# Hybrid decoder layer on one core: weight-side sums of the seven-product pairs formed by accumulating GpSimd transfers on a second loaded copy, with the signs of one K block turned

## The chip, the cores and the metric

The kernel runs on one core of one Trainium2 chip. The metric is the device time of one execution in microseconds (us). Of the kernel before there are three runs: 1558.5, 1558.77 and 1559.57 us; the median is 1558.77 us.

## What is computed

One layer of a hybrid decoder on 256 tokens of width 4096, in float32. RMS-normed input goes through one wide projection (4096 x 12288, the columns of `IN_ORDER`), whose columns feed three mixers: causal pooling, stick-breaking attention with 16 heads, and a diagonal state-space branch with a small gated linear unit. The three branch outputs are normed, gated and concatenated to `y` (256 x 4096), and one output projection closes the layer:

```python
h = rmsnorm(x, ln_g)
proj = h @ w_in
...
y = jnp.concatenate([y_pool, y_attn, y_ssm], axis=-1)
h = x + y @ w_out
return rmsnorm(h, final_g)
```

The change lies in the product `y @ w_out` alone.

## The kernel before

All weights are streamed once. The stream is cut into 528 steps (`subs`); a step is a block of 256 K rows by 512 columns, loaded by one 512 KB transfer on the SP queue into a tile `w` (128 partitions x 2 x 512, four buffers, `load`, L135 to L138). Each float32 weight is split into a high and a low part so that TensorE's fast float32 mode keeps the accuracy: ScalarE writes `hi` (L94 or L228), VectorE writes `lo = w - hi` (L82). Products are then formed as three matmuls: high x high, high x low, low x high (`mm_tok`, L234 to L239, for 512 columns).

The stage at the end, the output projection, has eight units of 512 columns with 16 steps each; the 256 x 256 blocks of `y` are the stationary operands. An ordinary step takes 12 matmuls of 512 columns. Five steps of each unit, those in `SEVEN`, go another way: the two K tiles of 128 rows and the two halves of 256 columns are taken as a 2 x 2 block product and formed with seven products in place of eight (a Winograd form of Strassen's scheme). Such a step takes 21 matmuls of 256 columns (`mm_seven`, L169 to L185), and needs

- four sums of weight blocks, formed by VectorE in `sums_seven` (three operations on L82: one of 128 x 512 and two of 128 x 256 elements) from the loaded tile `w`, and split into high and low parts `sums7` (one ScalarE and one VectorE operation of 128 x 1024);
- three sums of blocks of `y`, formed once in `sums_of_rows` before the stage;
- a joining of four PSUM pieces at the end of each unit's last such step (`join_seven`, L187 to L195), which adds them into the residual tile `xr`.

The loop over steps is software-pipelined by emission order: in step i it emits the load of step i + 4 (`LOAD_AHEAD`), the split of step i + 2 (`SPLIT_AHEAD`), for a seven-product step its sums one step ahead of its split, and then the matmuls of step i. The `hi` and `lo` tiles have five buffers each, that is two and a half steps. A scheduler then sets the order on each compute engine from a timeline model; the SP queue keeps the order in which the program was written. GpSimd has no work but four small constants.

The tiles `t` (sums), `xr`, `e` (joining) and some others share one ring of six 4 KB-per-partition buffers (tag `k4`); `sums7` and others share a ring of three of 8 KB (`k8`). In the last unit, the last four steps (`HELD`) keep their split weights: the matmuls of the first token half run first, and those of the second half (`delayed`) run while the first half is being normed and stored.

Of the kernel before, what the change touches and what calls it, by code (L numbers as in the profile page):

```python
# [19 lines left out]
P = 128  # L20
L = 256
# [10 lines left out]
HELD = 4  # L32
SUMS_AHEAD = 1
SEVEN = (2, 5, 7, 9, 11)
SQUARE_AT = (0, 1, 3, 4, 6, 7, 9, 10)
# [20 lines left out]
def body(tc, a, out, ctx):  # L56
    nc = tc.nc
    V, S, T = nc.vector, nc.scalar, nc.tensor

# [60 lines left out]

# [1 line left out]
    wtiles, htiles = {}, {}  # L122
    held = []
# [34 lines left out]
    def split_seven(i):  # L158
        w = wtiles.pop(i)
        raw = []  # L160
        for kk in range(2):
            n = L if kk == 0 else NU
            hi = wp.tile([P, NU], F32R, tag="hi", bufs=5, name="hi")
            lo = wp.tile([P, NU], F32R, tag="lo", bufs=5, name="lo")
            hi_lo(hi[:, 0:n], lo[:, 0:n], w[:, kk, 0:n])
            raw.append((hi, lo))
        htiles[i] = (raw, htiles[i])

    def mm_seven(i, s, ps, pp):  # L169
# [5 lines left out]
        for o, stat, mov, begin, end in (  # L175
            (pp[0], xa[:, :, lo_half], [v[:, 0:L] for v in b11], first, last),
            (ps[:, 0, 0:L], xb[:, :, lo_half], [v[:, 0:L] for v in b2], False, False),
            (ps[:, 0, L:2 * L], y[:, 2], [v[:, L:2 * L] for v in b2], False, False),
            (pp[1], y[:, 0], [sums[:, h, 0] for h in range(2)], False, last),
            (pp[3], xa[:, :, hi_half], [sums[:, h, 1] for h in range(2)], first, last),  # L180
            (pp[2], y[:, 1], [sums[:, h, 2] for h in range(2)], False, last),
            (ps[:, 1, 0:L], xb[:, :, hi_half], [sums[:, h, 3] for h in range(2)], False, False),
        ):
            for k, (p, q) in enumerate(((0, 0), (0, 1), (1, 0))):
                T.matmul(o, stat[:, p, :], mov[q], start=begin and k == 0, stop=end and k == 2, skip_group_check=True)  # L185
# [10 lines left out]
    def sums_of_rows(qp, srcs):  # L196
        state["s7"] = {}
        for s in SEVEN:
# [49 lines left out]

# [1 line left out]
    state = {}  # L250
# [28 lines left out]

# [1 line left out]
    def log1pexp_parts(z, l):  # L281
# [47 lines left out]

# [1 line left out]
    pool_sums = cp.tile([P, 2, 2], F32, name="pool_sums")  # L331
# [43 lines left out]

# [1 line left out]
    uT = bp.tile([P, 8, L], F32, tag="k8", bufs=3, name="uT")  # L377
# [206 lines left out]

# [1 line left out]
    aout = {}  # L586
# [66 lines left out]

# [1 line left out]
    cur = {}  # L655
# [31 lines left out]

# [1 line left out]
    units = []  # L689
# [76 lines left out]
    def finish(kind, c, n, ps):  # L766
# [64 lines left out]
        elif kind == "ag":  # L831
            z = scaled(ps, "agz")
            if n == 2:
                drain(side_q)
                att_ctx.close()
                qp = ctx.enter_context(tc.tile_pool(name="rows", bufs=1, reuse_waits="tile"))
                side_q.append(sums_of_rows(qp, y_src))
            side_q.append(att_gate(lp, n, z))
            if n == 3:
                for i in range(28):  # L840
# [19 lines left out]
    for i, (ui, s) in enumerate(subs):  # L860
# [10 lines left out]
        while loaded < min(len(subs), i + 1 + LOAD_AHEAD):  # L871
            if loaded == 0:
                load_first()
            else:
                if loaded < KT // 2:
                    load_x(loaded)
                load(loaded)
            loaded += 1
        while split_to < min(len(subs), i + 1 + SPLIT_AHEAD):
            split(split_to)  # L880
            split_to += 1
            if seven(split_to + SUMS_AHEAD):
                sums_seven(split_to + SUMS_AHEAD)
        if s == 0:
# [156 lines left out]
```

## Time and profile before

| | us |
|---|---|
| median of three runs | 1558.77 |
| span of the profiled execution | 1556.4 |
| TensorE matmul busy | 1538.2 |
| VectorE busy | 1201.6 |
| ScalarE busy | 913.9 |
| GpSimd busy | 0.2 |
| data moved by DMA | 308.45 MB, 198 GB/s on average |

The span runs from the first to the last instruction of the profiled execution; the median of the runs is 2.4 us longer than this span. TensorE's busy time counts a matmul from its start to the modelled end of its pipeline, so 99% of the span says that matmuls follow one another without gaps, not that the array does peak work. Busy time of the other engines is true occupation. The output projection begins at about 1200 us of the span and TensorE's last matmul ends at about 1545 us; the rest is norm and stores.

### The profile page before, as it was taken

Reading aid. Unit: us, or ns where it says so; the run is one execution under the profiler, and the core shown is the slowest. Engines: PE = TensorE matmul, PEld = TensorE weight load, DVE = VectorE, ACT = ScalarE, POOL = GpSimd, SP = SyncE. Lnnn points to the kernel's source line nnn. Section 1 sums busy time; section 2 is a strip of 40 time slices with the busy share of each in tenths; the row PEclk is TensorE's granted clock in tenths of the full one; section 3 lists DMA queues with packets and bytes.
Section 4 is the critical chain, followed back from the end, with each engine's and each line's share of the span. In section 5 each row is a group of like instructions: output and inputs, shape, how many; then the busy total and the mean of one; then the engine's idle time right before and its main releaser. Section 6 shows DMA issues by size and latency. Waiting matters only on the chain.

```text
span 1556.4 us, 25428 instructions
## 1 busy us (share of the span) xinstructions
PE 1538.2 (99%) x9164; PEld 1360.9 (87%) x9164; DVE 1201.6 (77%) x2325; ACT 913.9 (59%) x1637; POOL 0.2 (0%) x4
## 2 busy tenths in 40 slices
PE   8999999999999999999999999999999999999996
PEld 8998788888799989998998889988888888888885
DVE  7579978999898879897556745455678888888886
ACT  7655556666565555565546754456667655555554
POOL 0000000000000000000000000000000000000000
PEclk9999999999999999999999999999999999999999
DMA  8866656566655546554555555545556666666665
GB/s 320 306 214 205 195 162 205 186 206 194 205 188 185 187 156 197 176 175 162 183 186 180 180 185 183 183 159 186 190 178 193 212 220 220 216 214 210 204 222 198
DMA packets 94079, 308.45 MB, mean 198 GB/s; under 512 B 11777, under 2 KB 17665, under 8 KB 93953
## 3 DMA queue, kind: packets, MB, share of 16 engines
q1 hardware_dynamic: 84096, 296.08, 58.2%
q10 hardware_dynamic: 9856, 10.76, 2.3%
q8 instruction: 71, 1.16, 0.3%
q14 instruction: 56, 0.45, 0.1%
HBM read 299.45 MB, written 4.19 MB: 195 GB/s over the span
## 4 chain that ended last, share of the span: by engine, by line
PE 96%; DVE 2%; DMA 1%; ACT 1%; issue 0%; SPq 0%; DVEq 0%; ACTq 0%
PE pm L238 18%; PE pm L237 18%; PE pm L239 18%; PE pm L245 10%; PE pm L247 10%; PE pm L246 10%; PE ps L185 3%; PE pm L185 3%; DVE lo L82 1%; PE ps_y L572 1%; DMA w<-in_ws 1%; PE ps_bu L545 0%; ACT hi L228 0%; PE ps_z L598 0%; PE ps_p L356 0%; PE ps_t L296 0%
## 5 line engine op out<-in xcount | busy, mean ns | idle before, releaser
L82 DVE TENSOR_TENSOR lo<-w,hi 128x512 fp32r<-128x512 f32 (+1 forms) x1048 | 696.9, 678 | 273.1 <-ACT hi L228 266.0
L228 ACT ACTIVATE hi<-w 128x512 fp32r<-128x512 f32 x968 | 604.6, 629 | 503.2 <-PE pm L239 204.4
L238 PE MATMUL pm<-lo,xhl 128*128 128x512 f32 x1232 | 482.4, 392 | 0.0
L239 PE MATMUL pm<-hi,xhl 128*128 128x512 f32 x1232 | 480.8, 390 | 0.0
L237 PE MATMUL pm<-hi,xhl 128*128 128x512 f32 x1232 | 480.6, 390 | 0.0
L245 PE MATMUL pm<-xhl,hi 128*128 128x256 f32 x1280 | 363.8, 284 | 5.3 <-ACT xhl L94 5.3
L246 PE MATMUL pm<-xhl,hi 128*128 128x256 f32 x1280 | 363.5, 284 | 0.0
L247 PE MATMUL pm<-xhl,lo 128*128 128x256 f32 x1280 | 363.4, 284 | 0.0
L238 PEld LDWEIGHTS pm<-lo,xhl 128*128 128x128 f32 x1232 | 231.5, 188 | 48.9 <-issue 2.1
L239 PEld LDWEIGHTS pm<-hi,xhl 128*128 128x128 f32 x1232 | 231.4, 188 | 47.3 <-issue 1.2
L237 PEld LDWEIGHTS pm<-hi,xhl 128*128 128x128 f32 x1232 | 231.5, 188 | 46.9 <-issue 0.4
L245 PEld LDWEIGHTS pm<-xhl,hi 128*128 128x128 f32 x1280 | 246.6, 193 | 7.1 <-ACT xhl L94 5.3
L247 PEld LDWEIGHTS pm<-xhl,lo 128*128 128x128 f32 x1280 | 246.6, 193 | 1.2 <-issue 0.8
L246 PEld LDWEIGHTS pm<-xhl,hi 128*128 128x128 f32 x1280 | 246.6, 193 | 0.8 <-issue 0.4
L91 DVE SCALAR_TENSOR_TENSOR et<-et,pw,tr 128x16 f32<-128x16 f32 (+3 forms) x256 | 55.6, 275 | 2.3 <-ACT tr L94 1.9
L94 ACT ACTIVATE sums<-t 128x1024 fp32r<-128x1024 f32 x40 | 42.3, 1058 | 23.8 <-DVE t L82 23.3
L82 DVE TENSOR_TENSOR sums<-t,sums 128x1024 fp32r<-128x1024 f32 x40 | 48.9, 1223 | 8.8 <-ACT sums L94 8.7
L94 ACT ACTIVATE hi<-w 128x256 fp32r<-128x256 f32 x80 | 40.0, 518 | 22.4 <-PE pm L239 18.9
L185 PE MATMUL ps<-sums,s 128*128 128x256 f32 x240 | 46.5, 283 | 1.1 <-DVE sums L82 1.1
L94 ACT ACTIVATE tr<-et,pw 128x32 f32<-128x32 f32 (+3 forms) x128 | 44.7, 384 | 4.7 <-DVE et L91 2.0
L82 DVE TENSOR_TENSOR t<-w 128x512 f32<-128x512 f32 x40 | 27.6, 690 | 24.3 <-DMA w<-in_ws 24.0
L560 DVE TENSOR_TENSOR_SCAN tb<-rho,ta 128x256 f32<-128x256 f32 x64 | 40.6, 676 | 0.1
(258 smaller groups left out, 1261.3 us busy)
## 6 DMA issues: line engine op xcount, KB each, us to landing
w<-in_ws SPq DMA_DIRECT2D x527, 512.0 KB, 3.5
xsq<-in_xr SPq DMA_DIRECT2D x8, 512.0 KB, 7.2
xr<-in_xr SPq DMA_DIRECT2D x8, 512.0 KB, 4.5
out<-o SPq DMA_DIRECT2D x8, 512.0 KB, 4.0
xt<-in_xT SPq DMA_DIRECT2D x15, 256.0 KB, 6.1
b<-in_bst ACTq DMA_DIRECT2D x16, 192.0 KB, 3.6
u<-uT ACTq DMA_DIRECT2D x96, 32.0 KB, 3.0
fg<-in_fg SPq DMA_DIRECT2D x8, 256.0 KB, 5.9
```

Source lines behind the costliest of these rows:

```text
L82: V.tensor_tensor(o, x, y, op)
L91: V.scalar_tensor_tensor(o, x, s, y, op0, op1)
L94: S.activation(o, x, f, **kw)
L185: T.matmul(o, stat[:, p, :], mov[q], start=begin and k == 0, stop=end and k == 2, skip_group_check=True)
L228: made = S.activation(hi, w[:, kk, :], AF.Copy)
L237: T.matmul(ps[t], stat[:, slot, 0, sl], hi, start=first, stop=False)
L238: T.matmul(ps[t], stat[:, slot, 0, sl], lo, start=False, stop=False)
L239: T.matmul(ps[t], stat[:, slot, 1, sl], hi, start=False, stop=last)
L245: T.matmul(o, hi[:, c], xhl[:, slot, 0, :], start=first and j % 2 == 0, stop=False, skip_group_check=True)
L246: T.matmul(o, hi[:, c], xhl[:, slot, 1, :], start=False, stop=False, skip_group_check=True)
L247: T.matmul(o, lo[:, c], xhl[:, slot, 0, :], start=False, stop=last, skip_group_check=True)
L560: V.tensor_tensor_scan(tb[:, c, :], rho[:, pr:pr + 1].broadcast_to([P, L]), ta[:, c, :], 0.0, ALU.mult, ALU.add)
```

## The change

The four weight sums are no longer formed by VectorE. Each seven-product step loads its 512 KB weight block a second time, on the SP queue, straight into the tile `t7`, eight steps ahead of its use (`SUMS_LOAD_AHEAD`). Three transfers issued by GpSimd then accumulate in place, each waiting for the one before: the right half of the weight block from memory onto the first two quarters of `t7` (256 KB), quarter 0 onto quarter 3 (128 KB), and quarter 3 onto quarter 2 (128 KB). An accumulating transfer can only add, so the differences of the old form are turned into sums by turning the sign of one K block: the sums over `y` rows and the joining take the signs, by scalar_tensor_tensor in place of tensor_tensor at two places each. The split into `sums7` stays and moves into `split_seven`, two steps ahead of use. Quarters 2 and 3 change places.

The seven-product steps are still five in each unit, at other places: (1, 4, 7, 10, 13) in place of (2, 5, 7, 9, 11). The row sums of step 13 need an output of attention that is ready later, so they are formed one block later. In the last unit step 13 is one of the last four; it runs for both token halves at once, so the `delayed` work is that of three steps in place of four.

```diff
-SUMS_AHEAD = 1
-SEVEN = (2, 5, 7, 9, 11)
+SUMS_LOAD_AHEAD = 8
+SEVEN = (1, 4, 7, 10, 13)
...
-    def sums_seven(i):
-        w = wtiles[i]
-        left, right = w[:, :, 0:L], w[:, :, L:2 * L]
+    def load_sums(i):
         t = bp.tile([P, 4, L], F32, tag="k4", bufs=6, name="t7")
-        tt(t[:, 0:2, :], right, w[:, 0, :].rearrange("p (c m) -> p c m", c=2), ALU.subtract)
-        tt(t[:, 2, :], right[:, 1, :], t[:, 0, :], ALU.subtract)
-        tt(t[:, 3, :], left[:, 1, :], t[:, 2, :], ALU.subtract)
+        nc.sync.dma_start(t.rearrange("p q m -> p (q m)").rearrange("p (k n) -> p k n", k=2), a["ws"][i])
+        G.dma_start(t[:, 0:2, :], a["ws"][i][:, :, L:2 * L], accum_op=ALU.add)
+        G.dma_start(t[:, 3, :], t[:, 0, :], accum_op=ALU.add)
+        G.dma_start(t[:, 2, :], t[:, 3, :], accum_op=ALU.add)
+        stiles[i] = t
+
+    def split_sums(i):
         sums = bp.tile([P, 2, 4, L], F32R, tag="k8", bufs=3, name="sums7")
-        hi_lo(sums[:, 0], sums[:, 1], t)
-        htiles[i] = sums
+        hi_lo(sums[:, 0], sums[:, 1], stiles.pop(i))
+        return sums
...
-        htiles[i] = (raw, htiles[i])
+        htiles[i] = (raw, split_sums(i))
...
-            (pp[2], y[:, 1], [sums[:, h, 2] for h in range(2)], False, last),
-            (ps[:, 1, 0:L], xb[:, :, hi_half], [sums[:, h, 3] for h in range(2)], False, False),
+            (pp[2], y[:, 1], [sums[:, h, 3] for h in range(2)], False, last),
+            (ps[:, 1, 0:L], xb[:, :, hi_half], [sums[:, h, 2] for h in range(2)], False, False),
...
-        tt(e[:, 1, :], e[:, 3, :], pp[1], ALU.add)
+        stt(e[:, 1, :], e[:, 3, :], -1.0, pp[1], ALU.mult, ALU.subtract)
         tt(e[:, 2, :], e[:, 3, :], pp[3], ALU.add)
-        tt(e[:, 3, :], e[:, 2, :], pp[1], ALU.add)
+        stt(e[:, 3, :], e[:, 2, :], -1.0, pp[1], ALU.mult, ALU.subtract)
...
-            tt(t[:, 0, :], xa[:, P:L], xb[:, P:L], ALU.add)
-            tt(t[:, 1, :], t[:, 0, :], xa[:, 0:P], ALU.subtract)
-            tt(t[:, 2, :], xb[:, 0:P], t[:, 1, :], ALU.subtract)
+            tt(t[:, 0, :], xb[:, P:L], xa[:, P:L], ALU.subtract)
+            stt(t[:, 1, :], t[:, 0, :], -1.0, xa[:, 0:P], ALU.mult, ALU.subtract)
+            tt(t[:, 2, :], xb[:, 0:P], t[:, 1, :], ALU.add)
...
+        if seven(i + SUMS_LOAD_AHEAD):
+            load_sums(i + SUMS_LOAD_AHEAD)
         while split_to < min(len(subs), i + 1 + SPLIT_AHEAD):
             split(split_to)
             split_to += 1
-            if seven(split_to + SUMS_AHEAD):
-                sums_seven(split_to + SUMS_AHEAD)
```

Two places of the built order show the moves. The first is the SP queue in the first units of the output projection. Before, it held weight loads with the residual and the final norm's gain once per unit (`w`, `xr`, `fg`):

```order
L137 DMA w_14570<-in_ws 128x1024
L761 DMA xr_14587<-in_xr 128x1024
L763 DMA fg_14589<-in_fg 128x512
L137 DMA w_14612<-in_ws 128x1024
L137 DMA w_14634<-in_ws 128x1024
```

Now a second copy stands between the weight loads, one after every three or four of them (`t7`):

```order
L149 DMA t7_13627<-in_ws 128x1024
L137 DMA w_13655<-in_ws 128x1024
L137 DMA w_13677<-in_ws 128x1024
L762 DMA xr_13687<-in_xr 128x1024
L764 DMA fg_13689<-in_fg 128x512
L137 DMA w_13712<-in_ws 128x1024
L137 DMA w_13737<-in_ws 128x1024
L149 DMA t7_13739<-in_ws 128x1024
L137 DMA w_13764<-in_ws 128x1024
```

Nothing else on SP moved: the loads of `w` keep their order.

The second is GpSimd's queue in the same stage, which was empty. L150 adds the right half of the weight block, L151 quarter 0 onto quarter 3, L152 quarter 3 onto quarter 2; the number names the tile:

```order
L150 DMA t7_13739<-in_ws 128x2x256
L152 DMA t7_13627<-t7_13627 128x256
L151 DMA t7_13739<-t7_13739 128x256
L150 DMA t7_13822<-in_ws 128x2x256
L152 DMA t7_13739<-t7_13739 128x256
L151 DMA t7_13822<-t7_13822 128x256
L150 DMA t7_13909<-in_ws 128x2x256
L152 DMA t7_13822<-t7_13822 128x256
L151 DMA t7_13909<-t7_13909 128x256
L152 DMA t7_13909<-t7_13909 128x256
```

The scheduler has put the first addition of the next tile between the second and the third of the present one; once in a unit the second and third of one tile stand together. Each L151 and L152 waits for the landing of its own tile's addition before it.

More of the change, by code (lines that the diff above doesn't have):

```diff
@@ L57, in body @@
     nc = tc.nc
-    V, S, T = nc.vector, nc.scalar, nc.tensor
+    V, S, T, G = nc.vector, nc.scalar, nc.tensor, nc.gpsimd
     ctx.enter_context(tc.manual_schedule(engines={mybir.EngineType.SP}))
@@ L119, in rsqrt_mean @@
         stt(dst, t, 1.5, dst, ALU.add, ALU.mult)
-    wtiles, htiles = {}, {}
+    wtiles, htiles, stiles = {}, {}, {}
     held = []
@@ L190, in join_seven, with sums_of_rows @@
         tt(e[:, 3, :], e[:, 0, :], pp[2], ALU.add)
-        tt(e[:, 1, :], e[:, 3, :], pp[1], ALU.add)
+        stt(e[:, 1, :], e[:, 3, :], -1.0, pp[1], ALU.mult, ALU.subtract)
         tt(e[:, 2, :], e[:, 3, :], pp[3], ALU.add)
-        tt(e[:, 3, :], e[:, 2, :], pp[1], ALU.add)
+        stt(e[:, 3, :], e[:, 2, :], -1.0, pp[1], ALU.mult, ALU.subtract)
         tt(xr, xr, e.rearrange("p (t c) m -> p t (c m)", t=2), ALU.add)
-    def sums_of_rows(qp, srcs):
-        state["s7"] = {}
-        for s in SEVEN:
+    def sums_of_rows(qp, srcs, which):
+        for s in which:
             xa, xb = srcs(2 * s), srcs(2 * s + 1)
             t = qp.tile([P, 3, P], F32, tag="t", bufs=1, name="ts")
-            tt(t[:, 0, :], xa[:, P:L], xb[:, P:L], ALU.add)
-            tt(t[:, 1, :], t[:, 0, :], xa[:, 0:P], ALU.subtract)
-            tt(t[:, 2, :], xb[:, 0:P], t[:, 1, :], ALU.subtract)
+            tt(t[:, 0, :], xb[:, P:L], xa[:, P:L], ALU.subtract)
+            stt(t[:, 1, :], t[:, 0, :], -1.0, xa[:, 0:P], ALU.mult, ALU.subtract)
+            tt(t[:, 2, :], xb[:, 0:P], t[:, 1, :], ALU.add)
             tt(xa[:, P:L], xa[:, 0:P], xa[:, P:L], ALU.subtract)
@@ L836, in finish @@
                 qp = ctx.enter_context(tc.tile_pool(name="rows", bufs=1, reuse_waits="tile"))
-                side_q.append(sums_of_rows(qp, y_src))
+                state["s7"] = {}
+                side_q.append(sums_of_rows(qp, y_src, [s for s in SEVEN if s < 12]))
             side_q.append(att_gate(lp, n, z))
+            if n == 2:
+                side_q.append(sums_of_rows(qp, y_src, [s for s in SEVEN if s >= 12]))
             if n == 3:
```

## The prediction

> **What bounds the kernel now.** I read the page first (busy shares, queues, the chain that ended last), then the waits of TensorE, then the stage of the change by windows.
>
> ```profile
> span 1556.4 us, 25428 instructions
> PE 1538.2 (99%) x9164; PEld 1360.9 (87%) x9164; DVE 1201.6 (77%) x2325; ACT 913.9 (59%) x1637; POOL 0.2 (0%) x4
> ...
> q1 hardware_dynamic: 84096, 296.08, 58.2%
> q10 hardware_dynamic: 9856, 10.76, 2.3%
> ...
> PE 96%; DVE 2%; DMA 1%; ACT 1%; issue 0%; SPq 0%; DVEq 0%; ACTq 0%
> ```
>
> TensorE makes 96% of the chain that ended last. The waits that end at its matmuls, over the whole span, are three:
>
> ```profile
> engine line waited for: us in total, times, longest us
> PE pm L245 <- ACT xhl L94: 5.3, 1, 5.3
> PE ps L185 <- DVE sums L82: 1.1, 1, 1.1
> PE pm L237 <- DVE o L82: 0.8, 1, 0.8
> ```
>
> The 5.3 us are the first load. Only 1.1 us, once in 40 seven-product steps, is a wait for weight sums: relieving VectorE can win little more than this. Now the stage, in stretches of about one unit each, and ahead of them a stretch near the start of the kernel (columns: PE, PEld, DVE, ACT, POOL busy, clock, share of the DMA engines, GB/s):
>
> ```profile
> core 0: us, PE busy (x) PEld busy (x) DVE busy (x) ACT busy (x) POOL busy (x), PEclk, DMA share, GB/s
> 8.00:24.00 16.00, 16.00 (x126) 16.00 (x125) 14.21 (x28) 13.47 (x28) 0.00 (x0) 1.00 1.03 401
> 24.00:50.00 26.00, 26.00 (x219) 26.00 (x219) 18.96 (x35) 17.99 (x35) 0.00 (x0) 1.00 0.86 286
> ...
> 1374.00:1417.00 43.00, 43.00 (x240) 37.66 (x239) 36.03 (x60) 24.79 (x42) 0.00 (x0) 1.00 0.65 214
> ```
>
> In the unit, TensorE is busy without a gap, VectorE for 36 of 43 us, and the DMA engines move 214 GB/s at a share of 0.65. Near the start the engines are full (1.03; packets overlap a little) and move 401 GB/s, and TensorE has no gap there either: heavy traffic by itself does not slow it. 401 GB/s is my capacity. The next 26 us, 286 GB/s at 0.86, would be 286 / 0.86 = 333 GB/s when full; this is the low end.
>
> The length of a unit comes from one instruction that stands once in each but the last (the final gain):
>
> ```profile
> L82 DVE TENSOR_TENSOR o<-o,fg x7: 1224/1225/1228, 1248.7 to 1505.1; 128x1024 f32<-128x1024 f32 x7
> ```
>
> Six intervals from 1248.7 to 1505.1 make 42.7 us a unit, 2.67 us a step.
>
> **The change, part by part.** *TensorE* keeps its work: five seven-product steps a unit before and now. Nothing is removed there.
>
> *VectorE* loses three operations a step (rows of the last 310 us, seven of the eight units):
>
> ```profile
> L82 DVE TENSOR_TENSOR t<-w,t 128x256 f32<-128x256 f32 x70 | 29.3, 419 | 0.2
> L82 DVE TENSOR_TENSOR t<-w 128x512 f32<-128x512 f32 x35 | 24.2, 690 | 20.5 <-DMA w<-in_ws 20.3
> ```
>
> 690 + 2 x 419 = 1528 ns, times 40 is 61 us of VectorE; off the path, so worth between 0 and the 1.1 us above. Four operations of the joining and of the row sums change their form from tensor_tensor to scalar_tensor_tensor: same sizes, a few tens of ns, hidden by VectorE's 7 idle us in a unit. ScalarE keeps its work.
>
> *DMA* is where the change costs. What a unit moves now: 16 loads of 512 KB, `xr` 512 KB, `fg` 256 KB:
>
> ```profile
> w<-in_ws SPq DMA_DIRECT2D x101, 512.0 KB, 3.9
> xr<-in_xr SPq DMA_DIRECT2D x6, 512.0 KB, 4.5
> fg<-in_fg SPq DMA_DIRECT2D x6, 256.0 KB, 5.9
> ```
>
> That is 9.18 MB, over 42.7 us 215 GB/s, as the window says. Added are five copies of 512 KB, 2.62 MB, and five times 256 + 128 + 128 KB accumulated, another 2.62 MB. The trace holds no accumulating transfer, so its price per byte is open. From below: like a copy. Then a unit has 14.42 MB, 338 GB/s over 42.7 us, 84% of 401: hidden, at no cost. From above: an accumulation reads the source, reads the old destination and writes, and each counts as a copy, so three times. Its pieces are of 1 KB; the queue with pieces of that order (q10, 1.1 KB a packet) moves 10.76 / 2.3 = 4.7 MB per percent of the engines against 5.1 on q1, so 9% more per byte. Three times: 9.18 + 2.62 + 3 x 2.62 x 1.09 = 20.4 MB, at 401 GB/s 50.8 us a unit, 8.1 over 42.7, times eight units 65 us. I take twice, the middle: the two reads pass one engine, the write goes out beside them. 9.18 + 2.62 + 5.71 = 17.5 MB, 43.7 us a unit: 1.0 us over TensorE's time, 8 us in the stage. That holds if the engines stay as full as in the 401 row; at half way to the low end, 367 GB/s, it is 47.7 us and +40 us in all. I take 1.6 us a unit, 13 us, nearer to the 401 row, because work then stands at the engines all the time, as there.
>
> The Trainium skill, "Collectives: The Full Stack", section "The bandwidth ceiling", gives a rule against this change: a reduce on a DMA engine has two source reads for each chunk on the same read ring, and its rate is half that of a copy (32.35 against 62.28 GB/s measured there). By the rule the price is twice a copy, which is the middle that I took; no transfer in this trace shows it.
>
> *The chain of transfers* behind each tile: second copy, then three accumulations, one after the other. Landing times nearest to them are 3.9 us (512 KB, above) and that of small copies within the on-chip memory:
>
> ```profile
> u<-uT ACTq DMA_DIRECT2D x96, 32.0 KB, 3.0
> ```
>
> Four landings are 12 to 16 us. The lead: the copy is issued eight steps ahead in a loop whose splits run as far ahead of TensorE at issue as at use, so 8 x 2.67 = 21.4 us. Hidden while landings stay under about 5 us. ScalarE's split of `t7` waits for the last landing; behind it in ScalarE's queue stand the `hi` parts of the next steps, for them VectorE's `lo` and TensorE.
>
> GpSimd's queue is in order. In the built order a tile's second and third addition have the first of the next tile between them, so a tile holds the queue for about two landings, 6 to 7.8 us, against 42.7 / 5 = 8.5 us of spacing. Hidden, with little to spare.
>
> *SP* gets 40 more issues at 0.33 us each (ns, window of one unit):
>
> ```profile
> L137 SPq DMA_DIRECT2D w<-in_ws x17: 327/328/328, 1373.9 to 1416.9; - x17
> ```
>
> They stand in a queue that mostly waits for a free `w` buffer; weight loads behind a second copy start that much later, hidden by their own lead of four steps, 10.7 us, against 3.9.
>
> *The tail.* In the last unit TensorE's end is followed by the norm; the joining now comes two steps later:
>
> ```profile
> 1535.77 0.19 PEld L238 LDWEIGHTS pm<-held,xhl 128*128 128x128 f32 x1 [0.26 <-DVE held L82]
> ...
> 1536.57 1.22 DVE L82 TENSOR_TENSOR xr<-xr,e 128x1024 f32<-128x1024 f32 x1
> 1536.71 0.19 PEld L238 LDWEIGHTS pm<-held,xhl 128*128 128x128 f32 x1 [0.41 <-DVE held L82]
> ...
> 1537.51 0.39 PE L238 MATMUL pm<-held,xhl 128*128 128x512 f32 x1
> ...
> 1537.74 0.40 PE L239 MATMUL pm<-held,xhl 128*128 128x512 f32 x1
> ...
> 1538.85 0.69 DVE L82 TENSOR_TENSOR o<-pm,xr 128x512 f32<-128x512 f32 x1 [1.06 <-PE pm L239]
> 1539.60 0.19 PEld L237 LDWEIGHTS pm<-held,xhl 128*128 128x128 f32 x1 [1.21 <-DVE o L82]
> ```
>
> ```profile
> L82 DVE TENSOR_TENSOR e<-e,ps 128x256 f32<-128x256 f32 x28 | 11.1, 417 | 2.3 <-PE ps L185 2.0
> ```
>
> Two waits for a late `lo` (0.26 and 0.41 us) go with VectorE's relief. After step 13, two steps of six matmuls remain before the first half is read, 12 x 0.23 = 2.8 us (the two starts above); the joining takes one copy, four operations of 0.42 us and the 1.22 us above, some 3.3 us, of which the copy runs under the last matmuls. I put the tail at zero, between -0.7 and +1.
>
> Sum against the profiled execution: 1556.4 + 13 + 0 = 1569.4 us; the runs lie 2.4 us above the span (1558.77 - 1556.4): 1571.8, say **1572 us**.
>
> **The rivals.** *Everything stays hidden (not slower).* One mechanism: an accumulation costs the engines less than 1.8 copies. It decides at the point where a unit's transfers fit in 42.7 us at 401 GB/s, 17.1 MB: (17.1 - 11.8) / (2.62 x 1.09) = 1.86; a little less with imperfect filling. For it: engines at 0.65 and a lead of 21 us; against it: 84% fill already at the lowest price. It gives 1558.3 us, with the tail and the 1.1 us wait between 1556.5 and 1560.
>
> *GpSimd's queue paces the stage.* Under load, or by generating descriptors in software, a landing takes 5 us: two per tile are 10 us against 8.5, 1.5 x 40 = 58 us, less the lead left over (21.4 - 15 = 6): +52, 1611 us. It decides from 8.5 / 2 = 4.3 us a landing. For it: `fg` lands in 5.9 us already; against it: the small copies' 3.0. The same time would come from an accumulation of three copies' price (+65).
>
> The Trainium skill, "DMA: Bandwidth & Descriptors", section "Anatomy of one DMA", fits a GpSimd transfer with 2.0 us + bytes / 436 GB/s; an estimate by it is 2.3 us for 128 KB, which would keep this rival away. No run here shows it, so it moves nothing in the numbers.
>
> *The change is a gain.* Only TensorE's 1.1 us and the tail's 0.7 are to be had: at most 1.8 us, 1557, which this measurement could not tell from no change (it tells about 0.2%, 3.1 us).
>
> **How the numbers follow.** Forecast, engines just over full: 0.43, own range 1563 (+4) to 1599 (+40). Far slower by GpSimd's queue or a triple price: 0.16. Hidden: 0.41, of which 0.05 for a gain over 0.2% by something in the stage that I don't see, 0.36 within. Slower by over 0.2%: 0.43 + 0.16 = 0.59. The range runs from the hidden case's low end, 1556, to 1612, which leaves out the gain (0.05) and the upper half of the far slower case (0.08 to 0.1).
>
> **What would show it.** Right: the DMA share in the stage at or above 0.95; TensorE with gaps in the units that end at weight loads or at `sums7`; units of about 44 us between two `o<-o,fg`. VectorE's busy time down by 61 us. Wrong towards hidden: units of 42.7 us, share below 0.9. Wrong towards far slower: units of 48 us and more, ScalarE waiting for `t7`, and landings of the L151 and L152 transfers over 4.3 us with the DMA share below 0.9 (queue) or at 1 (price).

## The result, and the profile after

| | before | after |
|---|---|---|
| median of four runs each, us | 1559.17 | 1680.55 (1679.41 to 1681.67) |
| ratio, 95% interval | | 1.078 (1.0764 to 1.0795) |
| span of the profiled execution, us | 1556.4 | 1679.0 |
| length of a unit in the last stage, us | 42.7 | 58.1 |

The change costs 121 us, nine times the forecast of 13. The page of the changed kernel: the span, the busy times, three DMA queues and the engines' shares of the chain that ended last.

```profile
span 1679.0 us, 25805 instructions
...
PE 1578.6 (94%) x9164; PEld 1382.8 (82%) x9164; DVE 1151.4 (69%) x2205; ACT 905.6 (54%) x1637; POOL 113.9 (7%) x124
...
q1 hardware_dynamic: 89856, 317.06, 55.5%
q0 software_dynamic: 22400, 20.98, 8.3%
...
PE 73%; DMA 15%; issue 5%; DVE 3%; ACT 2%; POOL 1%; SPq 0%; DVEq 0%; ACTq 0%; POOLq 0%
```

TensorE's part of the chain falls from 96% to 73%; DMA rises from 1% to 15%. The unit is read, as before, from the instruction that stands once in each unit but the last:

```profile
L82 DVE TENSOR_TENSOR o<-o,fg x7: 1216/1225/1226, 1268.8 to 1617.5; 128x1024 f32<-128x1024 f32 x7
```

(1617.5 - 1268.8) / 6 = 58.1 us. Eight units at 15.4 us more are 123 us: the whole loss lies in this stage. Two stretches of it by windows (PE, PEld, DVE, ACT, POOL busy, clock, DMA share, GB/s):

```profile
1350.00:1400.00 50.00, 39.57 (x195) 32.49 (x194) 25.61 (x38) 20.23 (x37) 13.06 (x14) 0.90 0.86 236
...
1450.00:1500.00 50.00, 38.06 (x184) 31.62 (x182) 20.06 (x31) 17.04 (x30) 12.15 (x13) 0.90 0.86 241
```

Every compute engine idles, the DMA engines are busy but not full (0.86 here, 0.84 to 0.94 in the eight stretches of 50 us from 1250 to 1650). Nothing is at its limit: that is the look of a stage held by latency. The waits of TensorE, of ScalarE (1200 to 1660 us), of GpSimd (1300 to 1500 us) and of SP (1240 to 1620 us) say where it is held:

```profile
PE ps L187 <- ACT sums L94: 51.6, 10, 7.6
PE pm L238 <- ACT hi L229: 10.2, 9, 2.1
PE ps L187 <- ACT hi L94: 7.9, 5, 4.8
PE ps L187 <- DVE sums L82: 4.5, 12, 0.5
```

```profile
ACT sums L94 <- DMA t<-t: 152.5, 27, 11.0
```

```profile
POOL t L151 <- DMA t<-in_ws: 75.0, 17, 8.4
POOL t L152 <- DMA t<-t: 37.8, 14, 7.0
POOL t L150 <- DVE lo L82: 23.8, 6, 7.5
POOL t L150 <- DMA t<-in_ws: 7.3, 4, 3.0
```

```profile
SPq L137 <- DVE lo L82: 304.7, 96, 13.3
```

TensorE waits for the split sums, and ScalarE for the landing that the sums are split from. GpSimd waits for its own landings (L151 and L152), but at L150 also for a second copy: these waits, those put down to `lo` too, end some 0.6 us after the copy's landing. In most of them the copy was already under way; in one GpSimd came free 0.7 us before SP issued it. SP stands at a weight load L137 that waits for `lo` to free a `w` buffer, 304.7 us of 380. That as such is nothing new; the kernel before, between 1240 and 1550 us:

```profile
SPq L137 <- DVE lo L82: 196.2, 85, 5.3
SPq L137 <- DVE t L82: 44.0, 21, 4.0
```

What is new is the longest such wait, 13.3 us in place of 5.3. One tile in the timeline ties the engines together:

```profile
1387.29 1.04 SPq L149 DMA_DIRECT2D t<-in_ws  x1
...
1392.93 1.08 POOL L150 DMA_DIRECT2D t<-in_ws  x1 [1.95 <-DMA t<-in_ws]
...
1398.21 0.89 POOL L151 DMA_DIRECT2D t<-t  x1 [4.19 <-DMA t<-in_ws]
...
1405.69 1.28 POOL L152 DMA_DIRECT2D t<-t  x1
...
1407.70 14.45 SPq L137 DMA_DIRECT2D w<-in_ws  x3
...
1417.07 1.06 ACT L94 ACTIVATE sums<-t 128x1024 fp32r<-128x1024 f32 x1 [10.12 <-DMA t<-t]
1418.04 2.17 ACT L229 ACTIVATE hi<-w 128x512 fp32r<-128x512 f32 x4
1418.18 0.58 PE L187 MATMUL ps<-sums,s 128*128 128x256 f32 x1 [6.75 <-ACT sums L94]
1419.30 2.83 DVE L82 TENSOR_TENSOR lo<-w,hi 128x512 fp32r<-128x512 f32 x5
1422.32 0.38 SPq L149 DMA_DIRECT2D t<-in_ws  x1
```

From the copy's issue at 1387.29 to the split at 1417.07 are 29.8 us; the forecast had 12 to 16 for four landings. While ScalarE stands at this split for 10.1 us, the `hi` of the next steps stands behind it; `lo` follows `hi`; the three weight loads that begin at 1407.70 are through only at 1422.15, when `lo` has freed their buffers; and the next second copy stands behind them and goes out at 1422.32. A late tile delays the next copies: the chain is a closed loop. The ring of `t7` buffers has no part in it: SP waited 0.4 us for one between 1240 and 1620 us. The landings themselves (medians of the whole program, issue to landing, in us):

```profile
w<-in_ws SPq DMA_DIRECT2D x527, 512.0 KB, 3.6
t<-in_ws SPq DMA_DIRECT2D x40, 512.0 KB, 6.5
t<-in_ws POOLq DMA_DIRECT2D x40, 256.0 KB, 6.3
t<-t POOLq DMA_DIRECT2D x80, 128.0 KB, 4.9
```

### The profile page after: what moved, and what is told of

Same layout as the page of the kernel before. It is cut to its first block, busy times and chain, and to the rows that moved or that the text cites. A ratio compares the mean times of both kernels' runs of the same rounds, so it can differ in the third digit from the quotient of the medians.

```text
span 1679.0 us, 25805 instructions
## 1 busy us (share of the span) xinstructions
PE 1578.6 (94%) x9164; PEld 1382.8 (82%) x9164; DVE 1151.4 (69%) x2205; ACT 905.6 (54%) x1637; POOL 113.9 (7%) x124
## 4 chain that ended last, share of the span: by engine, by line
PE 73%; DMA 15%; issue 5%; DVE 3%; ACT 2%; POOL 1%; SPq 0%; DVEq 0%; ACTq 0%; POOLq 0%
PE pm L239 13%; PE pm L240 13%; PE pm L238 13%; DMA t<-t 10%; PE pm L246 9%; PE pm L248 9%; PE pm L247 9%; DMA t<-in_ws 6%; DVE lo L82 2%; PE ps_y L573 1%; ACT sums L94 1%; ACT hi L229 1%; POOL t L150 1%; PE ps L187 1%; DVE sums L82 1%
## 5 line engine op out<-in xcount | busy, mean ns | idle before, releaser
L238 PE MATMUL pm<-hi,xhl 128*128 128x512 f32 x1236 | 487.5, 395 | 10.2 <-ACT hi L229 10.2
L239 PE MATMUL pm<-lo,xhl 128*128 128x512 f32 x1236 | 488.8, 395 | 3.7 <-DVE lo L82 3.3
L240 PE MATMUL pm<-hi,xhl 128*128 128x512 f32 x1236 | 485.4, 393 | 0.0
L238 PEld LDWEIGHTS pm<-hi,xhl 128*128 128x128 f32 x1236 | 235.2, 190 | 61.3 <-ACT hi L229 13.6
L239 PEld LDWEIGHTS pm<-lo,xhl 128*128 128x128 f32 x1236 | 234.9, 190 | 56.8 <-DVE lo L82 8.6
L240 PEld LDWEIGHTS pm<-hi,xhl 128*128 128x128 f32 x1236 | 234.2, 189 | 48.3 <-issue 1.2
L150 POOL DMA_DIRECT2D t<-in_ws x40 | 47.5, 1189 | 1273.2 <-DVE lo L82 1227.2
L187 PE MATMUL ps<-sums,s 128*128 128x256 f32 x240 | 57.5, 331 | 56.1 <-ACT sums L94 51.6
L187 PEld LDWEIGHTS ps<-sums,s 128*128 128x128 f32 x240 | 43.3, 224 | 61.4 <-ACT sums L94 53.7
L94 ACT ACTIVATE hi<-w 128x256 fp32r<-128x256 f32 x80 | 39.3, 514 | 40.3 <-PE pm L240 27.7
```

The source lines that it names most:

```text
L94: S.activation(o, x, f, **kw)
L150: G.dma_start(t[:, 0:2, :], a["ws"][i][:, :, L:2 * L], accum_op=ALU.add)
L238: T.matmul(ps[t], stat[:, slot, 0, sl], hi, start=first, stop=False)
L239: T.matmul(ps[t], stat[:, slot, 0, sl], lo, start=False, stop=False)
L240: T.matmul(ps[t], stat[:, slot, 1, sl], hi, start=False, stop=last)
```

## The experiments

Three theories stood against each other. A, **the loop of latency**: the copy's issue is tied to the splits, so a chain of some 28 us must pass within the steps that the lead spans, and sets the pace. B, **the engines' price**: the added bytes fill the DMA engines. C, **GpSimd's queue**: two landings a tile in one in-order queue set the pace. Thirteen kernels were run; the kernel before took 1558.0 to 1558.1 us beside them.

**The places alone.** The kernel before, with the five steps at the new places:

```diff
-SEVEN = (2, 5, 7, 9, 11)
+SEVEN = (1, 4, 7, 10, 13)
...
-                side_q.append(sums_of_rows(qp, y_src))
+                side_q.append(sums_of_rows(qp, y_src, [s for s in SEVEN if s < 12]))
...
+            if n == 2:
+                side_q.append(sums_of_rows(qp, y_src, [s for s in SEVEN if s >= 12]))
```

> The kernel before with the seven-product steps at the new places (1, 4, 7, 10, 13) and the row sums of step 13 one block later; the weight sums stay on VectorE. All theories: the places cost nothing, 1557 to 1562 us. Over 1570 us would say that a part of the loss is the places and the tail.

Measured: 1559.41 us, ratio 1.0011 (1.0001 to 1.002). The places, the tail with them, cost about 1 us.

**The traffic alone.** All added transfers run, but nobody waits for them: `sums7` is split from the plain weight block.

```diff
-        hi_lo(sums[:, 0], sums[:, 1], stiles.pop(i))
+        hi_lo(sums[:, 0], sums[:, 1], w.rearrange("p k n -> p (k n)").rearrange("p (q m) -> p q m", q=4))
```

> All transfers stay as in the changed kernel, but nobody waits for them: the operands called sums are the split of the plain weight block (the sums of weights are left out of what is computed; ScalarE, VectorE and TensorE do operations of the same number and size). Theory A: without the wait the loop is open; only the engines' traffic is left, 1562 to 1595 us. Theory B: the traffic itself costs it, 1660 to 1690 us. Theory C: as A, 1562 to 1595 us, since a late GpSimd queue only holds free tiles.

Measured: 1595.07 us, ratio 1.024 (1.0225 to 1.0256). The transfers as such are worth 37 us, and 85 us go when the wait for the sums goes. Its unit, a window, its queues q1 and q0 between 1200 and 1570 us, and a wait of SP:

```profile
L82 DVE TENSOR_TENSOR o<-o,fg x7: 1217/1225/1226, 1257.4 to 1540.3; 128x1024 f32<-128x1024 f32 x7
```

```profile
1350.00:1400.00 50.00, 45.75 (x249) 39.50 (x248) 31.80 (x47) 24.76 (x45) 16.43 (x18) 0.97 1.05 304
```

```profile
q1 hardware_dynamic: 25593, 91.11, 67.3%
q0 software_dynamic: 20601, 19.30, 33.3%
```

```profile
SPq L149 <- DMA t<-t: 81.6, 15, 8.3
```

The unit is 47.2 us and the DMA share 1.05, over 1300 to 1500 us 1.01: the engines are full. But SP also waits 82 us for tiles that the third accumulation has not left, so B and C are not told apart by this run alone.

**Plain transfers.** The same run with the three GpSimd transfers as copies:

```diff
-        G.dma_start(t[:, 0:2, :], a["ws"][i][:, :, L:2 * L], accum_op=ALU.add)
-        G.dma_start(t[:, 3, :], t[:, 0, :], accum_op=ALU.add)
-        G.dma_start(t[:, 2, :], t[:, 3, :], accum_op=ALU.add)
+        G.dma_start(t[:, 0:2, :], a["ws"][i][:, :, L:2 * L])
+        G.dma_start(t[:, 3, :], t[:, 0, :])
+        G.dma_start(t[:, 2, :], t[:, 3, :])
```

> As e3 (nobody waits for the second copies and the three transfers; the sums of weights are left out of what is computed), but the three transfers copy in place of accumulating: same bytes, same queue, same pieces. If an accumulation costs the engines about twice a copy, a unit's traffic falls from 47.1 us by half of the GpSimd queue's third of it, to about 39 us, and hides under TensorE's 42.7: 1557 to 1567 us. If bytes alone count: as e3, 1590 to 1600 us.

Measured: 1563.38 us, ratio 1.0033 (1.002 to 1.0047); the unit is back at 42.6 us. The same queue between 1200 and 1530 us:

```profile
q0 software_dynamic: 6631, 19.78, 16.9%
```

As many bytes take the engines half the time: 19.78 MB are 16.9% of 330 us, 55.8 us; accumulated, 19.30 MB were 33.3% of 370 us, 123.2 us. An accumulation costs (123.2 / 19.30) / (55.8 / 19.78) = 2.3 copies of the same blocks. The copies go in longer pieces (3.0 KB a packet against 0.9), and no run separates the two; the forecast's price of twice with pieces of 1 KB, 2.18, is close. Of the 37 us, 32 go with accumulating, the shorter pieces included, 4 with the bytes and 1 with the places.

**No chain between the accumulations.** The traffic alone, the second and third accumulation with sources that no transfer writes:

```diff
-        G.dma_start(t[:, 3, :], t[:, 0, :], accum_op=ALU.add)
-        G.dma_start(t[:, 2, :], t[:, 3, :], accum_op=ALU.add)
+        G.dma_start(t[:, 3, :], xhl[:, 0, 0, :].bitcast(F32), accum_op=ALU.add)
+        G.dma_start(t[:, 2, :], xhl[:, 1, 0, :].bitcast(F32), accum_op=ALU.add)
```

> The run of the traffic alone (nobody waits for the sums, which are left out), with the second and third accumulation made independent: they take 128 KB each from a resident tile of y parts (the same for all tiles) instead of the quarter that the accumulation before has just written. Bytes, pieces and issues are the same; of the waits in GpSimd's queue only that for the second copy is left. In the run of the traffic alone the queue waited 270 of 386 us for its own landings, SP 82 us for a tile that these had not yet left, and the DMA share stood at 1.0: queue or engines. Queue: without the waits the stage goes at TensorE's own pace, 42.7 us a unit, 1560 to 1572 us. Engines' price of accumulation: the same bytes, 46 to 48 us a unit, 1588 to 1600 us.

Measured: 1602.56 us, ratio 1.0285 (1.027 to 1.03). Its GpSimd waits between 1300 and 1500 us, its unit, a window, and a place ahead of the stage:

```profile
POOL t L150 <- DMA t<-in_ws: 110.5, 18, 13.6
POOL t L150 <- issue: 26.3, 3, 12.9
...
```

```profile
L82 DVE TENSOR_TENSOR o<-o,fg x7: 1225/1226/1226, 1266.0 to 1546.1; 128x1024 f32<-128x1024 f32 x7
```

```profile
1350.00:1400.00 50.00, 47.14 (x244) 38.23 (x243) 29.51 (x44) 23.53 (x44) 14.41 (x15) 1.00 1.04 302
```

```profile
1213.51 0.42 ACT L94 ACTIVATE xhl<-ypT 128x256 fp32r<-128x256 f32 x1 [6.56 <-DMA t<-xhl]
```

GpSimd no longer waits for any of its own landings, only for second copies, and the unit still takes 46.7 us at a share of 1.04. So the 37 us are the engines' price, not the queue. The median lies above the expected 1588 to 1600 because the run has a cost of its own: the writing of `xhl` waits once for transfers that read it, and TensorE waits 11.8 us for that.

**Lead of 12.** One number of the changed kernel:

```diff
-SUMS_LOAD_AHEAD = 8
+SUMS_LOAD_AHEAD = 12
```

> One number is changed: the second copy is issued 12 steps ahead of use in place of 8. In the changed kernel a tile needs 27 to 28 us from the issue of its second copy to ScalarE's split, and a unit takes 58.1 us, so that 8 of its 16 steps are 29 us. Theory A, a loop of latency: the issue of the second copy is tied to the progress of the splits, and a unit cannot be shorter than 16/8 of the chain. With 12 steps the chain allows 28 / 12 x 16 = 37 us a unit, under TensorE's 42.7; then the DMA engines bind at about 45 us a unit: 1575 to 1600 us. Theory B, the engines' price: the accumulations fill the DMA engines and no lead helps: 1665 to 1690 us. Theory C, GpSimd's in-order queue spends two or more landings per tile, about 11.6 us: no lead helps either, 1660 to 1690 us.

Measured: 1651.81 us, ratio 1.0605 (1.0587 to 1.0623): 29 us less, and outside the ranges of all three theories. It is far less than half as much lead again should bring: 28.4 us of chain in 12 steps would be hidden even at TensorE's pace (12 x 2.67 = 32 us).

**Two additions on VectorE.** The chain is cut to one accumulation:

```diff
-        G.dma_start(t[:, 3, :], t[:, 0, :], accum_op=ALU.add)
-        G.dma_start(t[:, 2, :], t[:, 3, :], accum_op=ALU.add)
...
+        tt(t[:, 3, :], t[:, 3, :], t[:, 0, :], ALU.add)
+        tt(t[:, 2, :], t[:, 2, :], t[:, 3, :], ALU.add)
```

> The second and third accumulation (128 KB each) are replaced by two VectorE additions of 128 x 256 just ahead of the split; the second copy and the first accumulation stay. Theory A: the chain is one copy and one accumulation, 6.6 + 1.1 + 6.5 = 14 us, under the lead of 21.4: 1558 to 1565 us. Theory B: half of the accumulated bytes go, the engines are at 86% of a unit at TensorE's pace: 1558 to 1575 us. Theory C: one transfer per tile on GpSimd: 1558 to 1565 us. All three expect a cure; a time over 1600 us would speak against all.

Measured: 1661.93 us, ratio 1.0666 (1.064 to 1.0691). The chain from copy to split fell from 28.3 to 15.4 us, yet only 19 us were won. All three theories had expected a cure: as they stood, all three failed here. Its timeline shows what waits for what:

```profile
1365.05 0.88 DVE L82 TENSOR_TENSOR t<-t 128x256 f32<-128x256 f32 x2 [8.96 <-DMA t<-in_ws]
1365.85 0.68 DVE L82 TENSOR_TENSOR lo<-w,hi 128x512 fp32r<-128x512 f32 x1
...
1366.59 0.79 PE L240 MATMUL pm<-lo,xhl 128*128 128x512 f32 x1 [5.20 <-DVE lo L82]
1367.18 0.63 PE L241 MATMUL pm<-hi,xhl 128*128 128x512 f32 x1
1367.61 0.63 PE L239 MATMUL pm<-hi,xhl 128*128 128x512 f32 x1
```

TensorE does not wait for the sums here but for a `lo` of an earlier step, which stands behind the addition on VectorE. In the built order of VectorE (the numbers name the tiles; `w_14023` is the block of the additions' own step):

```
L82 TENSOR_TENSOR lo_13944<-w_13881,hi_13943 128x512
L82 TENSOR_TENSOR t7_13905<-t7_13905 128x256
...
L82 TENSOR_TENSOR t7_13905<-t7_13905 128x256
L82 TENSOR_TENSOR lo_13965<-w_13903,hi_13964 128x512
...
L82 TENSOR_TENSOR lo_14082<-w_14023,hi_14081 128x256
```

The blocks 13903, 13937, 13962 and 13993 are split between the additions and their own step: the scheduler's model had the transfer land early and put the additions four steps ahead. A place ahead of its own step eats the lead, since an in-order engine makes earlier splits, and through SP the next copies, wait for it. So theory A, amended after this run, has to count the lead in the built order, not in the source. The same holds for the run before this one, where the sums stand 2.7 steps ahead on average.

**One transfer, additions behind their own split.** The run with two additions on VectorE, and one order constraint a tile: the first addition comes behind the split of its own step.

```diff
+            own = hi_lo(hi[:, 0:n], lo[:, 0:n], w[:, kk, 0:n])
...
+        behind(V.tensor_tensor(t[:, 3, :], t[:, 3, :], t[:, 0, :], ALU.add), own[1])
```

> As e2 (one accumulation, then two VectorE additions), but the additions are held behind the split of the tile's own step in VectorE's order; in e2's built order they stand 3.5 steps too early on average. Theory A, now with the lead counted in the built order: the loop runs from the split that frees a weight buffer, through the issue of the second copy behind that buffer's load, to the sums. In e2 it has about 4 to 4.5 steps for a chain of 15.4 us, which makes 56 us a unit, as measured (56.1). Behind its own step it has 8.5 steps: 31 us a unit, under TensorE's 42.7; the DMA engines are at about 39 of 42.7 us: 1558 to 1570 us. Theory B, price of the transfers alone: as e2, 1650 to 1670 us.

Measured: 1572.33 us, ratio 1.0089 (1.0074 to 1.0104): 90 us less by the order alone, with the same transfers and operations, and 2 us above the range of theory A. The waits of its TensorE in the stage, and ScalarE's wait at the sums for a landing (1200 to 1600 us):

```profile
PE ps L196 <- DVE sums L142: 7.1, 8, 0.9
...
PE ps L196 <- ACT sums L141: 3.3, 7, 0.5
```

```profile
ACT sums L141 <- DMA t<-in_ws: 0.8, 4, 0.2
```

ScalarE hardly waits for a landing any more. TensorE's 10.4 us, no longer than 0.9 each, and the 1 us of the places make most of the 14 that are left.

**Lead 12, and the sums' split behind its own step's.** The same constraint on the changed kernel, on ScalarE and VectorE, and the lead:

```diff
-SUMS_LOAD_AHEAD = 8
+SUMS_LOAD_AHEAD = 12
...
+        one, two = hi_lo(sums[:, 0], sums[:, 1], stiles.pop(i))
+        behind(one, own[0])
+        behind(two, own[1])
```

> As e1 (all three accumulations, second copy 12 steps ahead), but the split of the sums is held behind the split of its own step on ScalarE and VectorE; in e1's built order it stands 2.7 steps too early. Theory A: 12.5 steps for a chain of 29 to 31 us make 37 to 40 us a unit, so the loop no longer binds, and what is left is the engines' traffic as in e3 (47 us a unit): 1588 to 1610 us. Theory B: as e1, 1645 to 1660 us. Theory C (GpSimd's queue spends two landings a tile): as e1 too.

Measured: 1622.28 us, ratio 1.0406 (1.0362 to 1.045). Better than each alone, but 27 us over the traffic alone, and between the range of theory A and that of B and C. GpSimd's waits between 1300 and 1500 us:

```profile
POOL t L159 <- DMA t<-in_ws: 65.5, 20, 9.6
POOL t L160 <- DMA t<-t: 64.1, 17, 6.8
...
POOL t L158 <- DVE lo L82: 2.4, 2, 2.3
```

Now the queue hardly ever lacks a copy (L158 waits 2.4 us), and the chain has grown to 39.2 us, 17.3 of them from the copy's issue to the first accumulation's: theory C could be at work here. GpSimd works or waits for its own landings nearly all the time, as the engine that sets the pace would.

**GpSimd in program order.** The changed kernel, GpSimd's queue kept as written, three accumulations of a tile in a row:

```diff
-    ctx.enter_context(tc.manual_schedule(engines={mybir.EngineType.SP}))
+    ctx.enter_context(tc.manual_schedule(engines={mybir.EngineType.SP, mybir.EngineType.Pool}))
```

> The changed kernel with GpSimd's queue in the order of the program: the three transfers of a tile follow one another, with none of the next tile between them. Theory A: the chain of a tile loses the waits behind the next tile's first transfer, but a tile's first transfer then waits behind the third of the one before; the chain stays within 2 us of 28: 1660 to 1695 us. Theory C: the interleaving is the cause, under 1610 us; or, if three landings in a row bind the queue, 3 x 6 = 18 us a tile, 90 us a unit, over 1850 us.

Measured: 1724.96 us, ratio 1.107 (1.1039 to 1.11). Worse by 44 us, in none of the ranges: the first accumulation of a tile now waits behind two landings of the tile before (copy to first accumulation 15.7 us instead of 8.6), and the chain is 33.5 us. So the interleaving of two tiles, which looked like a danger, was a help; what the queue adds to the chain does count, more than A allowed for.

**Two additions on VectorE, with a lead of 12.** The run of that name, and:

```diff
-SUMS_LOAD_AHEAD = 8
+SUMS_LOAD_AHEAD = 12
```

> The run with two VectorE additions in place of the two accumulations inside the tile, and its lead raised from 8 to 12 steps. In the built order the additions then stand about 7.5 steps ahead of their own step's split (3.5 at a lead of 8), so that the loop still spans only about 4 steps. Loop of latency, counted in the built order: 16/4 x 15.5 us = 62 us a unit, no better than at a lead of 8: 1650 to 1720 us. Loop of latency with the lead counted as the source has it (12 steps for 15.5 us, far under the 32 us that 12 steps of TensorE take): 1560 to 1575 us. Engines' price alone (the transfers are those of the run at a lead of 8): as that run, 1655 to 1668 us.

Measured: 1663.85 us, ratio 1.0678 (1.0646 to 1.0709). Four steps more of lead bought nothing: the scheduler moved the additions four steps further ahead (7.5). The count by the source's lead is refuted; the count by the built order gave 62 us a unit and 55.4 were measured, so its size is rough where additions and split stand at different places on two engines.

**Lead 8, sums behind.** The constraint alone on the changed kernel, the lead as it was:

```diff
+        behind(one, own[0])
+        behind(two, own[1])
```

> The changed kernel with its lead of 8, and the split of the sums held in the built order behind its own step's split on ScalarE and on VectorE (mean place 1.3 instead of 0.55). Loop of latency: the loop spans 8.8 steps instead of 8.05; with the chain of 28.3 us unchanged that is 53 to 54 us a unit, 1630 to 1670 us. Engines' price, or the order without a part in it: 1675 to 1686 us.

Measured: 1666.63 us, ratio 1.0694 (1.0671 to 1.0716), 54.6 us a unit, just over the 53 to 54 that A had.

**Lead of 6.** One number of the changed kernel:

```diff
-SUMS_LOAD_AHEAD = 8
+SUMS_LOAD_AHEAD = 6
```

> The changed kernel with a lead of 6 steps instead of 8, nothing else (mean place of the sums 1.45). Loop of latency: the loop spans about 7 steps; 16/7 x 29.3 us = 67 to 68 us a unit, 9 to 10 us more in each of eight units: 1740 to 1790 us. Engines' price: the same transfers, 1675 to 1690 us.

Measured: 1723.1 us, ratio 1.1085 (1.1045 to 1.1124), 64.2 us a unit. Slower as A had it, and by 17 us less than its low end: the transfers of a slower stage land sooner, and the chain was 25.1 us instead of 28.3.

**GpSimd's queue in rounds.** Lead 12 and the sums behind, GpSimd in program order, written so that no accumulation waits for one issued just before it:

```diff
...
         G.dma_start(t[:, 0:2, :], a["ws"][i][:, :, L:2 * L], accum_op=ALU.add)
-        G.dma_start(t[:, 3, :], t[:, 0, :], accum_op=ALU.add)
-        G.dma_start(t[:, 2, :], t[:, 3, :], accum_op=ALU.add)
+        if chain:
+            second(chain[-1])
+        if len(chain) > 1:
+            third(chain.pop(0))
+        chain.append(t)
...
```

> The run with a lead of 12 and the sums' split behind their own step's, with GpSimd's queue written in rounds: first accumulation of a tile, second of the tile before, third of the one before that, so that each waits for a landing that began a whole round earlier. Same transfers, same sums. In the run without rounds the queue never lacked work and gave 10.2 us a tile (51.2 us a unit). Queue paces that run: a round costs one landing, 8.5 us, instead of 10.2; 43 to 47 us a unit, 1565 to 1600 us. Engines' price: not under the run of the traffic alone, 1592 to 1625 us. Loop of latency alone: the chain grows by the rounds to some 40 us over a loop of 12.8 steps, 50 us a unit: 1615 to 1640 us, no gain.

Measured: 1632.39 us, ratio 1.0488 (1.0467 to 1.0508). GpSimd between 1300 and 1500 us:

```profile
POOL t L167 <- DMA t<-in_ws: 67.6, 9, 11.0
...
POOL t L158 <- DMA t<-in_ws: 0.7, 1, 0.7
```

At L167, the first accumulation, it waits for second copies (144 us of the 200 with the rows left out here), and no longer for its own landings (0.7 us), and nothing is won: a landing was traded for a wait in the round, and the chain is 39.3 us as before; the unit is 52.3 us against 51.2. So theory C does not set the pace of this run, nor that of the changed kernel: its queue was left without a copy at times, and with a lead of 6 the stage was slower though the queue had the same work. For the run with a lead of 12 and the sums behind it is not excluded: there the queue hardly lacked work, and this run, which frees the queue, adds a wait of its own to the chain.

**Seven runs in one reckoning.** In a closed loop, the chain passes once in as many steps as lie between the split that lets a copy go and the split that uses it. Those are the lead, plus the place of the sums' split in the built order (1 right behind its own step's split, negative ahead of it), less half a step; the half is set so that the changed kernel comes out. The chain is the mean over tiles 4 to 37 from the copy's issue on SP to the split on ScalarE, as in the timeline above (29.8 us for that tile), plus 1 us for the split. A unit is 16 steps.

| run | lead | place | steps | chain, us | 16 / steps x (chain + 1) | unit measured |
|---|---|---|---|---|---|---|
| after | 8 | 0.55 | 8.05 | 28.3 | 58.2 | 58.1 |
| lead 12 | 12 | -2.7 | 8.8 | 28.4 | 53.5 | 53.9 |
| lead 8, behind | 8 | 1.3 | 8.8 | 28.9 | 54.4 | 54.6 |
| lead 6 | 6 | 1.2 | 6.7 | 25.1 | 62.3 | 64.2 |
| GpSimd in turn | 8 | 1.05 | 8.55 | 33.5 | 64.6 | 64.5 |
| lead 12, behind | 12 | 1.0 | 12.5 | 39.2 | 51.5 | 51.2 |
| in rounds | 12 | 1.2 | 12.7 | 39.3 | 50.8 | 52.3 |

The place of the run with a lead of 6 is counted in the order of ScalarE's instructions in its trace (the expectation had 1.45). By the same count the runs with two additions on VectorE have places of -2.7 and, with a lead of 12, -6.0, and chains of 15.4 and 16.5 us: 54.7 and 50.9 us a unit, where 56.1 and 55.4 were measured. So for these two the reckoning is rougher.

The table can't show by itself that the chain sets the pace. The time from a copy's issue to its use is the number of steps between them times the length of a step, in every loop whose copies go out with the steps. The run with the additions behind their own split shows it: place 1.6, 9.1 steps, 23.2 us from copy to split, 42.5 us by the table's formula and 44.6 measured, though ScalarE did not wait there and the accumulation had landed 7.9 us before the split. That the chain binds is shown by ScalarE's waits for the landing (152.5 us against 0.8) and by the runs that changed the order or the lead alone. Why a chain is as long as it is, is left open: a chain grew where the lead grew (39 us at 12 steps), and no run separates, in it, the fuller engines from tiles that queue behind each other.

## Why the prediction was wrong, step by step

*TensorE bound, VectorE's relief worth nothing:* right. The three operations are gone, VectorE's busy total fell by 50.2 us (1201.6 to 1151.4; the sum of the removed durations was 61, and busy time counts instructions that overlap once), and nothing came of it. The four operations that changed form cost nothing: `e<-e,ps` takes 419 ns in the new form and 414 in the old.

*DMA, an accumulation at twice a copy:* the price was nearly right (2.3 measured against copies in longer pieces, 2.18 forecast with the pieces), the sum too small. The forecast was 13 us, from a unit of 44.3 us. The traffic alone gave 37 and 47.2 (with the run without a chain: 46.7). The term that was mis-sized is what full engines move: they were about as full as in the 401 row (shares of 1.01 and 1.04 over 1300 to 1500 us against 1.03), but 17.5 MB by the forecast's own count in 46.7 to 47.2 us are 371 to 375 GB/s, not 401. Both parts of the sum took more: an accumulated MB 6.4 us of the engines (123.2 / 19.30) where the forecast had 2.18 x 1.03 / 401 GB/s = 5.6, and a loaded MB 2.7 us (67.3% of 370 us for 91.11 MB) where it had 2.57. In a unit that is 2 us each, at 2.62 and 11.8 MB. The forecast's "half way to the low end, 367 GB/s, it is 47.7 us and +40 us" was the better value. The Trainium skill, "Collectives: The Full Stack", section "The bandwidth ceiling", has a reduce at half the rate of a copy because both its sources are read; the runs with and without accumulation come near it, at 2.3 against its 1.9 (62.28 / 32.35), the shorter pieces included.

*The chain of transfers:* the step that failed. "Four landings are 12 to 16 us. The lead ... 21.4 us. Hidden while landings stay under about 5 us." Three things were wrong in it. The landings were taken from rows of the kernel before (3.0 and 3.9 us), whose stage had a DMA share of 0.65, though the step before it had just filled the engines: by the medians the four took 6.5 + 6.3 + 4.9 + 4.9 = 22.6 us, over the lead already (in the mean of 28.3 us, 24.9 are landings). The waits between them on GpSimd and ScalarE, 3.4 us in that mean, were left out. And the lead was taken as a fixed time, out of which only the excess would be paid; but the copy is issued behind weight loads that wait for `lo`, and `lo` stands behind the late sums. In such a loop nothing is given back: the chain of 29.3 us sets 29.3 / 8.05 = 3.64 us for every step, where TensorE needs 2.67. These are 85 of the 121 us: the difference between the run of the traffic alone and the changed kernel.

*GpSimd's queue:* "Hidden, with little to spare" was wrong in the landings, and the rival that it fed (1611 us) was nearest to the result in size and not in its mechanism. Its condition, landings over 4.3 us, was met (4.9 and 6.3); but the queue of the changed kernel was itself left without a copy at times (L150, 23.8 + 7.3 of 200 us), the stage slowed when only the lead was cut to 6, and a queue without waits for its own landings (in rounds) was no faster than the one it was made from. The signs named ahead, "ScalarE waiting for `t7`" and "landings ... over 4.3 us with the DMA share below 0.9 (queue)", all came true, and would have been put down to the queue: the loop gives the same picture. GpSimd's L150 waits tell them apart, and the runs that changed the lead or the order and left the queue's work as it was; SP's L137 waits do not, since the kernel before has them too.

*SP:* the 40 issues were called hidden by the lead of the weight loads. Their own time is; but they stand in one queue with those loads, which is what ties the copy to the splits. *The tail:* right, within the 1 us of the places.

## What to carry to other kernels

A lead counted in steps is a time only as long as the steps keep their length. Where the prefetch is issued from a queue that waits for buffers which the consumer frees, ask what happens when the prefetch is late once: if its lateness delays the next issue, the price is the whole chain divided by the steps in the loop, not the excess over the lead. A time from issue to use that equals the lead proves nothing by itself; look whether the consumer waits for the landing. Read the place of the consumer in the built order, too: a scheduler that believes in an early landing puts it ahead on in-order engines and takes back the lead that the source gives (90 us lay in that in one of the pairs here).

## What the runs showed of the hardware

- An accumulating transfer in pieces of 1 KB took the DMA engines 2.3 times as long as plain copies of the same blocks in pieces of 3 KB (33.3% of 370 us for 19.30 MB against 16.9% of 330 us for 19.78 MB). How much of it is the size of the pieces, no run separates.
- Issuing a transfer took GpSimd 1.08 us for 256 KB (L150) and 0.86 us for 128 KB (L151), against 0.37 for a second copy of 512 KB on SP (L149), all medians of 40 in the changed kernel; single ones took longer (1.04 us for L149 and 1.28 for L152 in the timeline).
- TensorE's granted clock fell where its work had gaps: 0.90 in the two windows of the changed kernel against 1.00 before. After the wait of 5.20 us in the run with two additions on VectorE, matmuls started 0.43 us apart (1367.18, 1367.61), twice the 0.23 of the undisturbed stage. Over the whole kernel TensorE's busy time rose by 40.4 us (1538.2 to 1578.6) for the same 9164 matmuls, and its idle time by 82 us. So a third of the time lost shows as longer matmuls and not as waits; whether they lengthened the stage, or only filled what would have been waiting, no run separates.
